# The last block of a two-layer matmul: o5 as a fifth plain store, and o1 made on ScalarE

## Chip, cores, metric

One core of one Trainium2 chip. The metric is the time of the whole kernel on the device, in microseconds; lower is better. I also read the **tail** in each trace: the span minus the end of the last matmul. It leaves out the small drift of everything before. Spans are printed to 0.1 us, so a tail is good to about 0.1 us.

## The reference

```python
batch, m, k, h, n = 16, 512, 768, 3072, 768
def reference(x, w1, b1, w2):
    y = np.matmul(x, w1) + b1
    y = np.maximum(y, 0)
    return np.matmul(y, w2).astype(np.float32)
```

## The kernel before

The 8192 rows are worked through in 16 blocks, 8 for each half of the hidden dimension. The second product of a block consists of 20 small products ("mm") whose results are combined into eight outputs o0 to o7 of 128x768 floats (0.39 MB) each. In the first 8 blocks an output is stored; in the last 8 the second half's sum has to be added to what is stored. Usually the DMA does that: GpSimd issues an accumulating store. In the very last block, four outputs (`LAST`) go another way: the stored rows are fetched early, GpSimd adds them to a kept sum in SBUF, and the output then leaves as a plain store.

```python
SECOND = (            # ("mm", product, bank pair, start), (engine, to, bank pair, sign, kept, its sign)
    # [cut]
    ("mm", 10, 2, False),
    ("DVE", "q1", 2, 1, "s5", 1),
    ("DVE", "o5", 1, -1, "s2", 1),
    ("mm", 14, 0, False),
    ("ACT", "s4", 0, -1),
    ("mm", 9, 3, False),
    ("DVE", "q1", 3, -1, "s4", 1),
    ("DVE", "o7", 1, 1, "s1", -1),
    ("mm", 17, 2, False),
    ("DVE", "o4", 2, 1, "s5", 1),
    ("mm", 0, 0, False),
    ("DVE", "o1", 0, 1, "s3", -1),
    ("mm", 7, 3, False),
    ("DVE", "o6", 3, -1, "s4", 1),
)
# [cut]
    LAST = {"o7": ("s1", -1, 3), "o4": ("s5", 1, 15), "o1": ("s3", -1, 12), "o6": ("s4", 1, 16)}

    def fetch_last(self, to):
        slot = list(self.LAST).index(to)
        self.nc.sync.dma_start(out=self.x_outputs(slot), in_=self.rows_of(self.NIT - 1, to))

    def add_last(self, to):
        slot = list(self.LAST).index(to)
        name, sign, _ = self.LAST[to]
        s = self.s[:, int(name[1])].rearrange("p (a n) -> p a n", a=2)
        self.nc.gpsimd.tensor_tensor(out=s, in0=s, in1=self.x_outputs(slot),
                                     op=ALU.add if sign > 0 else ALU.subtract)
# [cut: total(), which combines one result]
            if final and to == SECOND[-1][1]:                     # o6, in two halves
                for j, queue in enumerate((nc.scalar, nc.sync)):
                    nc.vector.tensor_tensor(out=o[:, j], in0=at(kept)[:, j], in1=ps[:, j],
                                            op=ALU.subtract)
                    queue.dma_start(out=self.rows_of(it, to)[:, j], in_=o[:, j])
                return
# [cut]
            if to[0] == "o":
                rows = self.rows_of(it, to)
                if it < self.NSB or (final and to in self.LAST):
                    nc.sync.dma_start(out=rows, in_=o)
                else:
                    nc.gpsimd.dma_start(out=rows, in_=o, accum_op=ALU.add)
```

## Time and profile before

| | before |
|---|---|
| time, median of 3 runs | 880.64 us (880.54 to 880.95) |
| span of the profiled run | 879.4 us |
| last matmul ends | 870.62 us |
| last store issued | 872.89 us |
| DMA at full rate until | 876.0 us |
| DMA queues drained (SP's wait for the last store is over) | 878.5 us |
| tail (span less last matmul) | 8.8 us |

From the last matmul on, the table is the tail in order of time. Before it TensorE is at 98%. The lines of the page, of the timeline and of the DMA stretches are in the prediction below.

### The profile page before, as it was taken

The page shows a single profiled execution, that of the slowest core. Times are in us where ns is not written, and L with a number is a line of the kernel's source. Part 1 is how long each engine was busy: PE and PEld are TensorE (multiplying, and loading weights), DVE is VectorE, ACT ScalarE, POOL GpSimd, SP SyncE. Part 2 cuts the span into 40 slices and gives each one's busy share as a digit, 9 for nine tenths or more (in the row PEclk, how much of TensorE's full clock was granted, in tenths as well). Part 3 has the DMA queues.
Part 4 walks back from the last instruction along what each step waited for, and adds up shares of the span by engine and source line. Part 5 has one row for each costly group of instructions (what it writes and reads, how often), then busy time and mean ns, then how long its engine had stood idle before and what let it go on. Part 6 is the DMA issues. An engine that isn't in the chain of part 4 may idle for free.

```text
span 879.4 us, 12571 instructions
## 1 busy us (share of the span) xinstructions
PE 866.2 (98%) x4677; PEld 458.1 (52%) x4677; DVE 619.3 (70%) x1082; ACT 518.8 (59%) x791; POOL 193.3 (22%) x173
## 2 busy tenths in 40 slices
PE   8999999999999999999999999999999999999996
PEld 6454554645545455554545545455454555545453
DVE  2897857767677666866799676665866668566684
ACT  4865757768576776766356576775626345363541
POOL 6310150503305041040200402103030130401214
PEclk9999999999999999999999999999999999999998
DMA  9999598796977959549551837548263573726607
GB/s 206 197 224 273 109 251 219 136 264 148 280 161 190 255 91 268 122 179 337 224 180 55 129 102 167 89 137 133 86 118 67 149 121 126 102 43 162 108 1 146
DMA packets 121429, 139.68 MB, mean 159 GB/s; under 512 B 67196, under 2 KB 114836, under 8 KB 117524
## 3 DMA queue, kind: packets, MB, share of 16 engines
q0 software_dynamic: 49584, 44.83, 35.9%
q1 hardware_dynamic: 71312, 93.01, 32.3%
q10 hardware_dynamic: 468, 1.00, 0.4%
q8 instruction: 38, 0.62, 0.3%
q14 instruction: 27, 0.22, 0.1%
HBM read 73.74 MB, written 77.66 MB: 172 GB/s over the span
## 4 chain that ended last, share of the span: by engine, by line
PE 50%; issue 35%; POOL 9%; DVE 3%; DMA 2%; ACT 0%; POOLq 0%; DVEq 0%; ACTq 0%
PE ps L536 25%; PE ps L633 25%; POOL out_dram L685 8%; DVE v L338 1%; DMA v<-in_w_dram 1%; DMA w1s<-in_w_dram 1%; DVE y L468 1%; POOL s L618 1%; POOL w1s L277 1%; DVE o L678 0%; ACT ps L672 0%; DVE w1s L285 0%; DVE ps L678 0%; DVE x L678 0%; DVE x L391 0%
## 5 line engine op out<-in xcount | busy, mean ns | idle before, releaser
L633 PE MATMUL ps<-v,y 128*128 128x384 f16 x2560 | 424.6, 326 | 1.0 <-ACT ps L672 0.6
L536 PE MATMUL ps<-x,w1s 128*128 128x512 f16 x1890 | 415.6, 379 | 0.0
L633 PEld LDWEIGHTS <-y 128*128 128x128 f16 x2560 | 249.6, 98 | 173.0 <-ACT y L553 2.5
L536 PEld LDWEIGHTS <-w1s 128*128 128x128 f16 x1890 | 184.8, 98 | 218.6 <-issue 0.9
L544 ACT ACTIVATE s<-ps,b1y 128x512 f32<-128x512 f32 x210 | 142.1, 686 | 149.7 <-PE ps L536 69.2
L468 DVE TENSOR_TENSOR y<-y 128x512 f16<-128x512 f16 x512 | 203.2, 422 | 33.5 <-ACT y L553 26.0
L548 DVE CUSTOM_DVE_ANT_0 y<-ps,s 128x512 f16<-128x512 f32 x210 | 144.8, 690 | 102.8 <-PE ps L536 70.9
L672 ACT ACTIVATE s<-ps 128x768 f32<-128x768 f32 x96 | 77.7, 809 | 119.0 <-PE ps L633 106.7
L685 POOL DMA_DIRECT2D out_dram<-o x58 | 71.2, 1363 | 327.9 <-DVE o L678 327.9
L678 DVE TENSOR_TENSOR s<-ps,s 128x768 f32<-128x768 f32 x96 | 90.1, 952 | 11.6 <-ACT s L672 5.6
L678 DVE TENSOR_TENSOR o<-s,ps 128x768 f32<-128x768 f32 x54 | 51.3, 950 | 48.3 <-PE ps L633 25.9
L553 ACT ACTIVATE y<-ps,b1y 128x512 f16<-128x512 f32 x90 | 61.8, 687 | 39.7 <-PE ps L536 39.7
L678 DVE TENSOR_TENSOR o<-ps,s 128x768 f32<-128x768 f32 x55 | 51.3, 953 | 37.0 <-ACT s L672 35.1
L394 POOL TENSOR_TENSOR x<-x 128x3072 f16<-128x3072 f16 x7 | 42.0, 6004 | 65.2 <-DVE x L391 52.8
L382 ACT ACTIVATE scrap<-xn 128x768 f16<-128x768 f16 x60 | 50.3, 838 | 0.8
L277 POOL DMA_DIRECT2D x<-in_w_dram x12 | 10.1, 848 | 180.5 <-PE ps L536 92.9
L559 ACT ACTIVATE ps<-ps,b1y 128x512 f32<-128x512 f32 x60 | 39.5, 659 | 10.3 <-PE ps L536 7.6
L553 ACT ACTIVATE y<-ps 128x512 f16<-128x512 f32 x60 | 35.8, 597 | 0.0
L346 ACT ACTIVATE scrap<-scrap 128x1536 f16<-128x1536 f16 x24 | 35.4, 1476 | 0.1
L672 ACT ACTIVATE ps<-ps 128x768 f32<-128x768 f32 x32 | 25.5, 797 | 10.0 <-PE ps L633 8.4
L486 PE MATMUL ps<-x,w1s 128*128 128x512 f16 x132 | 28.8, 379 | 0.4 <-DVE x L441 0.2
L369 POOL DMA_DIRECT2D xn<-in_x_dram x15 | 11.5, 764 | 65.9 <-ACT scrap L382 65.2
(69 smaller groups left out, 288.5 us busy)
## 6 DMA issues: line engine op xcount, KB each, us to landing
out_dram<-o POOLq DMA_DIRECT2D x58, 384.0 KB, 5.9
out_dram<-o SPq DMA_DIRECT2D x51, 384.0 KB, 4.8
xd<-x SPq DMA_DIRECT2D x8, 1536.0 KB, 6.1
x<-xd SPq DMA_DIRECT2D x8, 1536.0 KB, 8.2
xn<-in_x_dram POOLq DMA_DIRECT2D x15, 768.0 KB, 7.2
xd<-x SPq DMA_DIRECT2D x7, 1152.0 KB, 8.0
x<-xd SPq DMA_DIRECT2D x7, 1152.0 KB, 5.3
out_dram<-x SPq DMA_DIRECT2D x16, 384.0 KB, 5.9
```

Source lines behind the costliest of these rows:

```text
L382: self.nc.scalar.activation(out=self.junk(self.K), in_=rows, func=ACTF.Square, accum_out=self.stat[:, i:i + 1])
L394: (self.nc.gpsimd if it > 1 else self.nc.vector).tensor_tensor(out=x[:, a21:self.XS2 + 1:self.XS2 - a21], in0=x[:, a21:self.XS1 + 1:self.X ...
L468: self.nc.vector.tensor_tensor(out=pair(*outs), in0=pair(*ins0), in1=pair(*ins1), op=ALU.add if sign > 0 else ALU.subtract)
L536: nc.tensor.matmul(ps, lhsT=w[:, slot, k, :], rhs=x[:, xslot, k, :], start=(start and k == 0), stop=(k == 2), skip_group_check=True)
L544: nc.scalar.activation(out=kept(name), in_=ps, func=ACTF.Identity, bias=bias)
L548: nc.vector._custom_dve(TENSOR_ADD_SAT, out=self.y_of(self.TP * half + t, m), in0=self.two(ps), in1=self.two(kept(name)), s0=F_MAX, s1=0.0)
L553: nc.scalar.activation(out=self.y_of(self.TP * half + t, m), in_=self.two(ps), func=ACTF.Relu, **kw)
L559: nc.scalar.activation(out=g["b"], in_=g["a"], func=ACTF.Identity, bias=bias1)
L633: nc.tensor.matmul(self.ps[:, 2 * q + j, 0:NH], lhsT=self.y[:, U_OF[p], m0:m0 + P], rhs=self.v[:, V_OF[p], s, :], start=(start and s == 0) ...
L672: nc.scalar.activation(out=o, in_=ps, func=ACTF.Copy, scale=float(sign))
L678: nc.vector.tensor_tensor(out=o, in0=a, in1=b, op=ALU.add if sign == kept_sign else ALU.subtract)
L685: nc.gpsimd.dma_start(out=rows, in_=o, accum_op=ALU.add)
```

## The change

Its intent: o5 becomes a fifth output that leaves by a plain store, so that no accumulating DMA stands among the last stores; and o1's kept sum is put into its banks of PSUM, the memory that TensorE writes to, before its last product, so that idle ScalarE can copy o1 out and store it from its own queue, and VectorE has one output less at the end.

```diff
-    LAST = {..., "o6": ("s4", 1, 16)}
+    LAST = {..., "o6": ("s4", 1, 16),
+            "o5": ("s2", 1, 5)}
@@ total()
-                    nc.sync.dma_start(out=rows, in_=o)
+                    (nc.scalar if final and to == "o1" else nc.sync).dma_start(out=rows, in_=o)
@@ second()
-        for what in SECOND:
+        order = list(SECOND)
+        if final:
+            at_s4 = order.index(("ACT", "s4", 0, -1))
+            order.insert(at_s4 + 1, ("DVE", "q0", 0, 1, "s3", -1))
+            order[order.index(("DVE", "o1", 0, 1, "s3", -1))] = ("ACT", "o1", 0, 1)
+        for what in order:
@@ plan()
-            put("m1", NIT - 1, 1, 6, self.fetch_last, to)
+            put(*(("m2", NIT - 1, 0, 1) if to == "o5" else ("m1", NIT - 1, 1, 6)),
+                self.fetch_last, to)
```

More of the change, by code (lines that the diff above doesn't have):

```diff
@@ L604, in x_outputs @@
         return o.rearrange("p (a n) -> p a n", a=2)
-    LAST = {"o7": ("s1", -1, 3), "o4": ("s5", 1, 15), "o1": ("s3", -1, 12), "o6": ("s4", 1, 16)}
+    LAST = {"o7": ("s1", -1, 3), "o4": ("s5", 1, 15), "o1": ("s3", -1, 12), "o6": ("s4", 1, 16),
+            "o5": ("s2", 1, 5)}
     def fetch_last(self, to):
```

## The prediction

> **What bounds the kernel now.** I read the page first, then the end of the timeline, then the waits there, then the DMA by stretches. The page says that TensorE is busy for 98% of the span, and the two costliest groups, the matmuls of the two products, have almost no idle time before them:
>
> ```profile
> PE 866.2 (98%) x4677; PEld 458.1 (52%) x4677; DVE 619.3 (70%) x1082; ACT 518.8 (59%) x791; POOL 193.3 (22%) x173
> ...
> L633 PE MATMUL ps<-v,y 128*128 128x384 f16 x2560 | 424.6, 326 | 1.0 <-ACT ps L672 0.6
> L536 PE MATMUL ps<-x,w1s 128*128 128x512 f16 x1890 | 415.6, 379 | 0.0
> ```
>
> The change touches nothing before the last of the 16 blocks' second product, so 843 us of the 879.4 us span are out of its reach, and within that product TensorE is fed without a gap (2.00 of 2.00 us in each stretch from 845 us to 869 us). What is left to gain is what comes after the last matmul. The timeline of the last 16 us shows it (start, duration, engine, line, what is written and read, count, idle time before):
>
> ```profile
> 864.95 1.21 POOL L685 DMA_DIRECT2D out_dram<-o  x1 [1.64 <-DVE o L678]
> 865.52 0.81 ACT L672 ACTIVATE s<-ps 128x768 f32<-128x768 f32 x1 [1.85 <-PE ps L633]
> 865.76 0.95 DVE L678 TENSOR_TENSOR o<-s,ps 128x768 f32<-128x768 f32 x1
> 866.85 0.96 DVE L678 TENSOR_TENSOR ps<-s,ps 128x768 f32<-128x768 f32 x1
> 867.01 1.20 POOL L685 DMA_DIRECT2D out_dram<-o  x1 [0.85 <-DVE o L678]
> 867.77 4.04 POOL L618 TENSOR_TENSOR s<-s,x 128x768 f32<-128x768 f32 x2
> 867.91 0.96 DVE L678 TENSOR_TENSOR o<-ps,s 128x768 f32<-128x768 f32 x1
> 868.90 3.41 SPq L683 DMA_DIRECT2D out_dram<-o  x3
> 870.09 1.82 DVE L678 TENSOR_TENSOR o<-ps,s 128x768 f32<-128x768 f32 x2 [1.22 <-POOL s L618]
> 871.85 1.02 DVE L666 TENSOR_TENSOR o<-s,ps 128x384 f32<-128x384 f32 x2
> 872.43 0.38 ACTq L668 DMA_DIRECT2D out_dram<-o  x1
> 872.89 0.34 SPq L668 DMA_DIRECT2D out_dram<-o  x1
> ```
>
> The last matmul ends at 870.6 us. GpSimd is the late one: it issues output o5 as an accumulating DMA at 867.01, and only then begins its two sums (o4's at 867.77, o6's after it, ending at 871.81). VectorE waits 1.22 us for the first, then does o4 and o1, then the two halves of o6, which end at 872.87. The last store goes out at 872.89, and 6.5 us later the span ends. These 6.5 us are DMA:
>
> ```profile
> 871.00:872.00 1.00, 0.00 (x0) 0.00 (x0) 1.00 (x3) 0.00 (x0) 0.81 (x1) 1.00 1.14 244
> 872.00:873.00 1.00, 0.00 (x0) 0.00 (x0) 0.87 (x2) 0.00 (x0) 0.00 (x0) 0.85 1.12 393
> 873.00:874.00 1.00, 0.00 (x0) 0.00 (x0) 0.00 (x0) 0.00 (x0) 0.00 (x0) 0.50 1.01 370
> 874.00:875.00 1.00, 0.00 (x0) 0.00 (x0) 0.00 (x0) 0.00 (x0) 0.00 (x0) 0.50 1.04 370
> 875.00:876.00 1.00, 0.00 (x0) 0.00 (x0) 0.00 (x0) 0.00 (x0) 0.00 (x0) 0.50 0.96 349
> ```
>
> The last two columns are the DMA share and GB/s. The engines are full until 876 at about 370 GB/s, then some lag until 877.5; the queues drain at 878.5 and the span ends 0.9 us later. By queue over the last 14 us (packets, MB, share of 16 engines' time):
>
> ```profile
> q0 software_dynamic: 544, 0.79, 40.9%
> q1 hardware_dynamic: 960, 1.38, 28.1%
> ```
>
> q0 holds GpSimd's two accumulating DMAs (o0, o5): 0.409 x 14 / 2 = 2.9 us of all 16 engines for one output. q1 holds plain stores of 1.38 MB: 0.281 x 14 = 3.9 us, so 1.1 us for one output of 0.39 MB. In half-microsecond stretches, o7's plain store, issued at 868.90, has its first packets only after 871, and the accumulating queue holds the engines until then. So the end is bound twice over: by o6's sum reaching VectorE late, and by four plain stores (1.57 MB) that queue up behind o5's accumulation.
>
> **What the Trainium skill says.** DMA: Bandwidth & Descriptors, section "SWDGE vs HWDGE vs iDMA", has an accumulating DMA go through GpSimd and a plain one through SP or ACT; the trace agrees (all L685 are POOL). The same page, "Issuing engines are not separate DMA queues", says that transfers from any issuer end on the same 16 engines, so that a second issuer saves only issuing time. The trace agrees: while both hardware queues run, the rate stays at 370 GB/s. I therefore give the second queue no bandwidth. The same page, "Anatomy of one DMA", gives some 2 us of fixed cost, mostly the receipt of the last write; here it is about 1 us from the last packets (877.5) to the drain, and from issue to first data 1.1 to 1.5 us (ACT's store issued at 872.43 has first packets between 873.5 and 874). SBUF — State Buffer, "Who interferes with whom", says that a VectorE instruction with two SBUF inputs and a GpSimd one that reads SBUF block each other, while one with a single SBUF input does not. The trace agrees: an f16 sum beside GpSimd's sum at 848.4 took 2.03 us in place of 0.4, while the PSUM-reading sum at 867.91 kept its 0.96.
>
> **The change part by part.** Orders and semaphores are read from the built programs.
> - Removed: the accumulating issue of o5 on GpSimd (1.2 us there, 2.9 us of all DMA engines).
> - Added early: one fetch of o5's rows (0.39 MB), free to go when the last block's first x-quarter is read, about 839 us, when DMA is idle; and one GpSimd sum of 1.9 to 2.3 us after step 5, near 854.5 us, where GpSimd is idle until 856.8. It may block the one f16 sum at 854.38 for 1.6 us; VectorE is idle 2.49 us before 859.0 and absorbs it. Cost: 0.
> - Added late: VectorE's sum of s3 into bank pair 0, between o5 and "q1 = s4 - q3". Sums with nothing to wait for start 0.87 us apart (854.71, 855.58), so it runs 866.65 to 867.6, q1 to 868.5, o7 868.6 to 869.5 (0.65 us later than now). The matmuls of product 0 now wait for it: 20 products of 1.31 us end at 870.62, so product 0 is due at 868.0 and product 7, which waits for q1, at 869.3. Slack 0.4 and 0.8 us: no TensorE cost.
> - Moved: o1 leaves VectorE (0.95 us) for ScalarE, idle since 866.3: product 0 ends at 869.3, so o1 is made 869.45 to 870.25 (0.80 us) and issued by ACT near 870.3, in place of 871.9.
> - GpSimd: o4's sum no longer stands behind o5's issue. It starts about 865.9 (after "q1 = q2 + s5" at 865.73) and ends near 868.1; o6's starts when q1 is made, 868.55, and takes 2.27: 870.8.
> - VectorE's end: o4 869.4 to 870.4, o6's halves 870.85 to 871.4 and to 871.9. Now 872.87: about 1.0 us earlier.
> - DMA: o5's plain store at 866.8 shares the engines with the rest of o0's accumulation and is through about 871. Then o7 (869.6), o1 (870.3), o4 (870.45), o6 (871.5, 871.95). First data of o7 is due 1.3 us after its issue, 870.9, where now it is about 871.6; four outputs at 370 GB/s are 4.25 us, so full rate ends near 875.2 in place of 876.0. Gain 0.7 to 0.8.
>
> The two ends (last issue 1.0 earlier, engines free 0.75 earlier) leave about 0.9 us; the laggards after 876 may shrink a little too, since those still full of accumulation at 871 are gone. 880.64 - 0.95 = 879.7 us.
>
> **The rivals.** (1) The drain hides it: five plain stores still need 5.3 us of the engines after 866.8, and if the o0 accumulation (landing about 870.3) holds o5's store back, the four last stores start no earlier than now. For it: o7 waited 2.6 us behind o5's accumulation today. Against it: the plain store takes 1.7 us less of the engines. Result 880.3 to 880.6. (2) The new wait on TensorE: if VectorE's sum into the banks ends after 868, the last products shift. For it: the slack is only 0.4 us, against semaphore delays of about 0.1. Even a 0.5 us shift of TensorE would be covered in part, as o6's sum arrives 0.2 us after its last matmul; result about 880.0. (3) More gain: with no accumulation in the last 6 us, the last store lands in the least time seen for such stores (2.4 us to landing against 4.3 to 5.1 here). Then the end comes at 871.95 + 3 + 1 = 876, which would need 1.57 MB faster than 370 GB/s; I allow up to 2 us in all, 878.7.
>
> **Range and chances.** The centre is 879.7. Rival 1 sets the upper end, 880.4; rival 3 the lower, 878.8. Two per cent would be 17.6 us, twice all the time after the last matmul (8.8 us), so faster is out of reach; slower would need a stall nowhere in the orders. Same 0.98, faster 0.01, slower 0.01.
>
> **What would show it.** Last matmul unmoved at 870.6 (right for the slack); the new sum into ps ending before 868; ScalarE's o1 near 869.5; no VectorE wait on GpSimd for o4; o6's halves ending near 871.9; the first plain-store packets before 871 and full rate ending near 875.2; the span near 878.4. Wrong if the last matmul comes later, if o6 still waits past 871.5 for GpSimd, or if VectorE ends earlier but the DMA drain doesn't.

## The result, and the profile after

The changed kernel takes 879.85 us (879.60 to 880.07, 6 runs) where the one before took 880.91 (880.54 to 881.34, 6 runs): 1.06 us less. The ratio is 0.9988 with a 95% interval of 0.9975 to 1.0001, so within 2% beyond doubt, and by the times alone not quite clear of zero. A ratio is the mean time of one kernel's fast runs over that of the other's of the same rounds, so not quite the ratio of the medians quoted.

The trace is clearer: span 878.2 us, last matmul at 870.71 (845.85 + 24.86, against 870.62), so the tail went from 8.8 to 7.5 us.

The end of the timeline of the changed kernel (start, duration, engine, line, out and in, count, idle time before). L679 is what L678 was, L619 what L618 was, L684 and L669 the stores:

```profile
865.97 2.13 POOL L619 TENSOR_TENSOR s<-s,x 128x768 f32<-128x768 f32 x1
866.78 0.96 DVE L679 TENSOR_TENSOR ps<-ps,s 128x768 f32<-128x768 f32 x1
866.90 3.97 SPq L684 DMA_DIRECT2D out_dram<-o  x3
867.65 0.95 DVE L679 TENSOR_TENSOR ps<-s,ps 128x768 f32<-128x768 f32 x1
868.64 1.82 DVE L679 TENSOR_TENSOR o<-ps,s 128x768 f32<-128x768 f32 x2
868.74 1.82 POOL L619 TENSOR_TENSOR s<-s,x 128x768 f32<-128x768 f32 x1 [0.64 <-issue]
869.45 0.81 ACT L673 ACTIVATE o<-ps 128x768 f32<-128x768 f32 x1 [3.03 <-PE ps L634]
870.29 0.50 ACTq L684 DMA_DIRECT2D out_dram<-o  x1
870.60 1.02 DVE L667 TENSOR_TENSOR o<-s,ps 128x384 f32<-128x384 f32 x2
871.18 0.37 ACTq L669 DMA_DIRECT2D out_dram<-o  x1
871.64 0.34 SPq L669 DMA_DIRECT2D out_dram<-o  x1
```

GpSimd begins o4's sum at 865.97, not 867.77, and VectorE no longer waits for that sum. The new sum into the banks is the one at 866.78. ScalarE makes o1 at 869.45. o6's halves end at 871.62, not 872.87, and the last store goes out 1.25 us earlier.

The stretches of the changed kernel (from left: window, its length, busy us and count of TensorE's matmuls, its weight loads, VectorE, ScalarE and GpSimd; TensorE's clock, DMA share, GB/s; the share is the time of all packets over that of 16 engines and can pass 1):

```profile
869.00:870.00 1.00, 1.00 (x8) 0.61 (x7) 1.00 (x2) 0.55 (x1) 1.00 (x1) 1.00 1.09 289
870.00:871.00 1.00, 0.71 (x5) 0.20 (x2) 0.87 (x2) 0.26 (x1) 0.56 (x1) 1.00 0.96 355
...
874.00:875.00 1.00, 0.00 (x0) 0.00 (x0) 0.00 (x0) 0.00 (x0) 0.00 (x0) 0.62 0.89 313
875.00:876.00 1.00, 0.00 (x0) 0.00 (x0) 0.00 (x0) 0.00 (x0) 0.00 (x0) 0.50 0.28 36
```

Full rate begins near 869.5 in place of 872 and ends near 874.8 in place of 876.0. The queues over the last 12.2 us of the changed kernel (q0 is GpSimd's, q1 SP's, q10 ScalarE's):

```profile
q1 hardware_dynamic: 960, 1.38, 33.2%
q0 software_dynamic: 272, 0.39, 24.4%
q10 hardware_dynamic: 416, 0.59, 13.6%
```

One accumulating output is left on q0 (o0: 0.244 x 12.2 = 3.0 us of all engines), and five plain ones are on q1 and q10. The drain ends at 877.3 and the span at 878.2.

Two explanations fit this: GpSimd, and so VectorE and the last issue, came free earlier; or the DMA engines did. And two halves of the change could have done it. The experiments take these apart.

### The profile page after: what moved, and what is told of

The parts are those of the page before. It is cut to its first block, busy times and chain, and to the rows that moved or that the text cites. A ratio compares the mean times of both kernels' runs of the same rounds, so it can differ in the third digit from the quotient of the medians.

```text
span 878.2 us, 12581 instructions
## 1 busy us (share of the span) xinstructions
PE 867.0 (99%) x4677; PEld 458.9 (52%) x4677; DVE 619.5 (71%) x1082; ACT 519.6 (59%) x792; POOL 194.0 (22%) x173
## 4 chain that ended last, share of the span: by engine, by line
PE 91%; DVE 4%; DMA 2%; POOL 1%; issue 1%; ACT 1%; DVEq 0%; POOLq 0%; ACTq 0%
PE ps L536 46%; PE ps L634 45%; DVE y L468 1%; DVE v L338 1%; DMA v<-in_w_dram 1%; DMA w1s<-in_w_dram 1%; POOL w1s L277 1%; DVE o L679 0%; DVE y L548 0%; POOL s L619 0%; ACT ps L673 0%; DVE ps L679 0%; ACT s L544 0%; ACT y L553 0%; DVE w1s L285 0%
## 5 line engine op out<-in xcount | busy, mean ns | idle before, releaser
L679 DVE TENSOR_TENSOR s<-ps,s 128x768 f32<-128x768 f32 x96 | 90.2, 954 | 11.5 <-ACT s L673 5.6
L679 DVE TENSOR_TENSOR o<-s,ps 128x768 f32<-128x768 f32 x54 | 51.4, 952 | 48.3 <-PE ps L634 25.9
L679 DVE TENSOR_TENSOR o<-ps,s 128x768 f32<-128x768 f32 x54 | 50.4, 953 | 35.7 <-ACT s L673 35.1
L277 POOL DMA_DIRECT2D x<-in_w_dram x12 | 10.1, 848 | 180.8 <-PE ps L536 92.6
```

What stands on the lines that cost most here:

```text
L679: nc.vector.tensor_tensor(out=o, in0=a, in1=b, op=ALU.add if sign == kept_sign else ALU.subtract)
```

## The experiments

Eleven builds ran, two of them repeats, in three groups of one chip each, all with five timed runs and one trace. The tail is worked out as above.

| kernel | time, us (range) | ratio, 95% interval | span | tail |
|---|---|---|---|---|
| before | 880.64 (880.54 to 880.95) | | 879.4 | 8.8 |
| changed | 879.85 (879.60 to 880.07) | 0.9988 (0.9975 to 1.0001) | 878.2 | 7.5 |
| group 1: after_again | 879.81 (879.56 to 879.98) | 0.9987 (0.9974 to 1.0001) | 878.3 | 7.4 |
| o5_plain | 879.26 (879.07 to 879.54) | 0.9982 (0.9968 to 0.9996) | 877.6 | 7.0 |
| act_o1 | 880.57 (880.15 to 880.77) | 0.9995 (0.9982 to 1.0009) | 878.9 | 8.2 |
| one_queue | 879.59 (879.52 to 880.09) | 0.9986 (0.9973 to 1.0000) | 878.0 | 7.3 |
| group 2: accum_last | 882.40 (882.01 to 882.68) | 1.0019 (1.0005 to 1.0032) | 881.0 | 10.1 |
| no_o7_store (wrong) | 879.55 (879.34 to 879.94) | 0.9989 (0.9975 to 1.0002) | 877.8 | 7.2 |
| pool_late | 879.71 (879.68 to 879.86) | 0.9991 (0.9977 to 1.0004) | 878.1 | 7.4 |
| o7_late | 879.84 (879.81 to 880.02) | 0.9992 (0.9978 to 1.0006) | 878.3 | 7.7 |
| group 3: o5_plain_again | 879.34 (879.27 to 879.52) | 0.9983 (0.9970 to 0.9997) | 877.8 | 7.1 |
| two_queues | 879.60 (879.30 to 879.90) | 0.9986 (0.9973 to 1.0000) | 877.9 | 7.2 |
| o0_plain | 879.31 (879.12 to 879.64) | 0.9983 (0.9969 to 0.9996) | 877.7 | 7.0 |

The kernel before ran beside each group: medians 880.93, 880.71 and 880.77, single runs from 879.82 to 881.55. Group 2 held neither the changed kernel nor o5_plain, and group 3 not the changed kernel; where I compare across groups, I rest on the tail more than on the times.

### after_again: the changed kernel as yardstick

No edit.

> The changed kernel once more, on the chip of this group, as the yardstick. It should be 0.9 to 1.2 us under the kernel before (ratio near 0.9988), with the same end as in its first trace: VectorE's last half of o6 done near 871.6, last store issued near 871.6, span 878.2.

It came as expected: 879.81 us, tail 7.4. The two traces of the changed kernel differ by 0.1 us in the tail, and so do those of o5_plain, below; with the rounding of the spans I read nothing into less than 0.2.

### o5_plain: only the first half of the change

```diff
+            "o5": ("s2", 1, 5)}          # and its fetch; SECOND and the queues as before
```

> The kernel before with o5 alone turned into a plain store (its fetch and its GpSimd sum too); o1 stays on VectorE and all stores on the SP queue. Theory 1 (the gain comes from taking the accumulating DMA of o5 away): GpSimd's sums for o4 and o6 start near 866.0 and 868.0, VectorE ends o6 near 871.6, span 878.2 to 878.4, so at least 0.8 us of the gain of about 1.1. Theory 2 (the gain comes from ScalarE taking o1 off VectorE): VectorE, with one more sum behind product 0, ends at 872.5 or later and the span stays above 879.0.

Theory 1 holds, and by more than it said: this half alone is faster than the whole change. Its ten runs in two groups lie at 879.07 to 879.54, the eleven of the whole change at 879.56 to 880.07. Timeline of this version, VectorE (o7, o4 and o1, then o6's halves):

```profile
867.93 2.69 DVE L679 TENSOR_TENSOR o<-ps,s 128x768 f32<-128x768 f32 x3
870.54 1.01 DVE L667 TENSOR_TENSOR o<-s,ps 128x384 f32<-128x384 f32 x2
```

VectorE makes o1 too and ends o6 at 871.55, no later than with ScalarE's help (871.62). It needed none: its three outputs stand there without a gap, and product 0 was due then anyway. The stretches of this version:

```profile
870.00:871.00 1.00, 0.65 (x4) 0.20 (x2) 1.00 (x3) 0.00 (x0) 0.00 (x0) 1.00 1.07 401
...
874.00:875.00 1.00, 0.00 (x0) 0.00 (x0) 0.00 (x0) 0.00 (x0) 0.00 (x0) 0.50 0.76 244
```

In 870 to 871 the engines move 401 GB/s, against 355 in the changed kernel, and by 874 to 875 there is less left to move (244 against 313).

### act_o1: only the second half

```diff
-            "o5": ("s2", 1, 5)}          # o5 accumulates again; the rest of the change stays
```

> The changed kernel with o5 accumulated as before: only the kept sum put into the banks, o1 made on ScalarE and stored from its queue. Theory 1: VectorE still waits for GpSimd (o4 near 870.1, o6 near 871.8), the last store goes out near 872.9, and the span stays within 0.3 us of 879.4. Theory 2: VectorE ends about 0.9 us earlier and the span is 878.5 or less.

VectorE's part came as theory 1 said: o4 at 870.21 after a wait for GpSimd, o6's halves at 871.97, last issue 873.01. The span was 878.9, and the 0.3 us around 879.4 that I gave it was too narrow; the tail is 0.6 us shorter than before. The median is 0.36 us under that of the kernel before, with an interval on both sides of 1: unclear. The trace says how a gain could come without an earlier last issue: o1's store went out at 870.31 in place of 871.94, so the engines had it in their queue sooner. The halves do not add: 1.7 to 1.8 us (tail) for the first, 0.6 for the second, 1.3 to 1.4 for both.

### one_queue: the changed kernel with o1's store on SP

```diff
-                    (nc.scalar if final and to == "o1" else nc.sync).dma_start(out=rows, in_=o)
+                    nc.sync.dma_start(out=rows, in_=o)
```

> The changed kernel with o1's store issued by SP in place of ScalarE's queue; nothing else. If the second queue adds no bandwidth (theory 1): span within 0.3 us of the changed kernel's 878.2, DMA rate in the full stretch still about 370 GB/s. If the second queue carries the gain (theory 3): the rate or the start of o1's data suffers and the span goes back by 0.5 us or more.

Span 878.0, tail 7.3: the second queue carries none of the gain. The rate at 871 to 874 was 354 to 366 GB/s, against 353 to 374 with two.

### pool_late: VectorE and the last issue as late as before, the DMA work as after

```diff
+        if to == "o6":                    # a useless sum ahead of o6's, in add_last()
+            f = self.x.rearrange("p a k m -> p a (k m)")
+            self.nc.gpsimd.tensor_tensor(out=f[:, 6, 0:1024], in0=f[:, 6, 0:1024],
+                                         in1=f[:, 7, 0:1024], op=ALU.add)
```

> The changed kernel with a useless GpSimd sum of 1.5 to 2 us ahead of o6's sum, so that o6's halves reach VectorE about 1.3 us later and nothing else moves. If the end follows the last issue: the span grows by 1.3 us, to 879.5. If it follows the drain: the engines have four other outputs to write until about 873.7, and o6's data could start only near 874.2, so it grows by 0.4 to 0.8 us.

This is the run that decides. Its timeline:

```profile
867.73 2.43 POOL L620 TENSOR_TENSOR x<-x 128x1024 f16<-128x1024 f16 x1
...
869.81 2.10 POOL L623 TENSOR_TENSOR s<-s,x 128x768 f32<-128x768 f32 x1
...
871.94 1.02 DVE L671 TENSOR_TENSOR o<-s,ps 128x384 f32<-128x384 f32 x2 [1.50 <-POOL s L623]
...
872.99 0.34 SPq L673 DMA_DIRECT2D out_dram<-o  x1
```

GpSimd is late again, VectorE waits 1.50 us for it, and the last store goes out at 872.99, 2.29 us after the last matmul; in the kernel before it was 2.27. What the change had won for o6 and for the last issue is taken back, and the span is 878.1, the tail 7.4, the time 879.71 (1.00 under the kernel before of its group; the whole change 1.06): nothing is lost. Both theories expected a loss, the drain theory 0.4 to 0.8 us. Its own stretches show why there is none:

```profile
873.00:874.00 1.00, 0.00 (x0) 0.00 (x0) 0.00 (x0) 0.00 (x0) 0.00 (x0) 1.00 1.11 381
874.00:875.00 1.00, 0.00 (x0) 0.00 (x0) 0.00 (x0) 0.00 (x0) 0.00 (x0) 1.00 0.84 282
```

There is no gap: the engines were still at full rate with the other outputs when o6 arrived, so its lateness is hidden entirely. **The earlier o6 and the earlier last store were worth nothing; the gain lies in when the DMA engines come free.** One thing the run leaves as the change made it: o4's store goes out at 870.47 and o1's at 870.27, in place of 871.07 and 871.94. Whether GpSimd's earlier sum for o4 helped, by having that store queued in time, no run tests by itself; o7_late, below, shows that a late store can cost.

### accum_last: the other way round

```diff
+                elif final and to == "o5":
+                    self.late = (rows, o)
@@ plan()
+        put("m2", NIT - 1, 0, 16, self.store_late)   # the same accumulating store, behind o6's sum
```

(store_late() issues the held store.)

> The kernel before with one move: GpSimd issues o5's accumulating DMA behind its two last sums in place of ahead of them. This frees GpSimd as the plain store did and leaves the DMA work where it was. If the end follows VectorE's last sum (6.5 us from the last issue to the end): VectorE ends near 871.5 and the span is near 878.1. If the end follows the drain of the DMA engines: VectorE ends near 871.5 all the same, but the accumulation, issued near 870, now falls among the last stores; 4.2 us of plain stores and 2.9 us of accumulation from about 869.7 end near 876.8, so the span is 879.4 to 880.2, no better than before.

The kernel before, with GpSimd freed and the accumulation left. VectorE ends o6 at 871.78 and the last store goes out at 871.80, as early as in the changed kernel. The kernel is 1.7 us slower than before (882.40 against 880.71 in its group; interval clear of 1), of which the tail shows 1.3. The direction is the drain theory's, the size over its 880.2. Its stretches show the cost of an accumulation among the last stores, full share at a low rate; a smaller part of the loss is a gap ahead of the plain stores (share 0.24 from 869.5 to 870.0), where the accumulation had stood before:

```profile
872.00:873.00 1.00, 0.00 (x0) 0.00 (x0) 0.00 (x0) 0.00 (x0) 0.00 (x0) 1.00 1.03 137
873.00:874.00 1.00, 0.00 (x0) 0.00 (x0) 0.00 (x0) 0.00 (x0) 0.00 (x0) 1.00 0.99 217
```

### no_o7_store: one store less

```diff
+                if final and to == "o7":
+                    return
```

> The changed kernel with the store of o7 left out: its rows keep the first half's sum, so the result is wrong on purpose. It takes 0.39 MB, 1.06 us at 370 GB/s, from the last DMA work and nothing from any compute engine. If the end follows the drain: the span shortens by 0.7 to 1.1 us, to about 877.3. If it follows the last issue: it stays at 878.2 within 0.2.

Between the two: span 877.8, tail 0.2 to 0.3 us shorter than the two of the changed kernel. Taking out a whole output's 1.06 us gave less than a third of it, because the engines then ran dry:

```profile
870.00:871.00 1.00, 0.65 (x4) 0.19 (x2) 0.87 (x3) 0.19 (x1) 0.49 (x1) 1.00 0.46 169
```

o5 was nearly all written by 870.5, and o1's store, issued at 870.22, had its first packets only after 871. So the drain is not just a sum of bytes: it also counts whether a store is in the queue when the engines come free.

### o7_late: what the second half costs

The version with only o5 plain, with o7's store behind o4's.

```diff
+                if final and to == "o7":
+                    self.held = (rows, o)
...
+                    if final and to == "o4":
+                        nc.sync.dma_start(out=self.held[0], in_=self.held[1])
```

> The version with only o5 plain (0.5 us faster than the whole change), with o7's store issued right behind o4's, near 870.2 in place of 868.9; compute is the same. In the whole change the sum put into the banks makes o7 0.65 us later. If that lateness is what the ScalarE half costs: the span goes from 877.6 to 878.0 or more, time near 879.7. If the cost has another cause (the second queue, ScalarE itself): the span stays within 0.2 of 877.6.

o7's store goes out at 870.21 in place of 868.9; VectorE's last sum is where it was (871.49). Time 879.84 and span 878.3, as the first theory said. The stretch shows the hole:

```profile
870.00:871.00 1.00, 0.60 (x4) 0.15 (x2) 1.00 (x3) 0.00 (x0) 0.00 (x0) 1.00 0.72 261
```

A late o7 is enough to lose 0.5 us (0.6 to 0.7 in the tail, against the two traces of o5_plain in the other groups). In the whole change o7's store goes out at 869.6, because the sum into the banks stands ahead of it on VectorE. The hole there is smaller (355 GB/s, share 0.96), so this run shows the mechanism, not that all of the 0.5 us is owed to it.

### o5_plain_again and two_queues

No edit for the first; for the second, on the same version:

```diff
-                    nc.sync.dma_start(out=rows, in_=o)
+                    (nc.scalar if final and to == "o1" else nc.sync).dma_start(out=rows, in_=o)
```

> The version with only o5 plain, once more, as the yardstick of this group and to see whether its lead over the whole change holds on another draw: about 879.3 us (ratio 0.998), span near 877.6. If it was a lucky chip or build: near 879.8.

> The version with only o5 plain, with o1's store (still made on VectorE) issued from ScalarE's queue as in the whole change. If the second queue is neutral: within 0.2 us of the yardstick. If two rows with work make the drain slower: 0.2 us or more above it. If they add bandwidth: below it, with more than 400 GB/s in the full stretch.

The lead of o5_plain held (879.34). With o1's store on the second queue it was 879.60. That is 0.26 us more, over the 0.2 from which I would have called the second queue slower, but single runs overlap and the tails differ by 0.1 us. Together with one_queue (0.22 us better with one queue, ranges overlapping too): two queues gain nothing; whether they cost 0.2 us stays open.

### o0_plain: no accumulating store issued after 861 us

```diff
+            "o5": ("s2", 1, 5), "o0": (None, 1, None)}
+            if final and to == "q1" and q == 2 and engine == "ACT":
+                nc.vector.tensor_tensor(out=o, in0=ps, in1=self.x_outputs(5), op=ALU.add)
+            elif kept is None:
```

(Cut: o0's fetch, placed as o5's, and no GpSimd sum for it.)

> The version with only o5 plain, with o0 made a plain store as well: its rows are fetched early and VectorE, idle there, adds them where ScalarE had only copied the seed of bank pair 1. No accumulating DMA is left after 861. Drain theory: o5's data no longer waits for o0's accumulation (starts near 868.2 in place of 869.3), but the four last stores are then limited by their own issue (o7 868.9), so full rate ends near 874.0 in place of 874.2 and the span shortens by 0 to 0.3 us. If the engines that lag by some 2 us at the very end owe it to accumulation behind them: it shortens by 1 us or more.

879.31 us, no different from o5_plain. Full rate does end a little earlier (112 GB/s in 874 to 875 in place of 244), but the queues drain at 876.8 as there (876.7). A whole accumulation less gained nothing, because the engines then ran dry ahead of o7, whose store goes out at 868.96:

```profile
869.00:870.00 1.00, 1.00 (x8) 0.59 (x6) 1.00 (x2) 0.00 (x0) 0.83 (x1) 1.00 0.14 52
```

Some engines still lag by about 2 us, so the lag is not owed to accumulations behind them. Which engines these are, the profile doesn't show; the cause stays open.

## Why the prediction was right

Predicted 879.7 us (878.8 to 880.4), measured 879.85; the predicted gain was 0.95 us, the measured one 1.06. Its steps:

- **TensorE has slack for the new wait.** Right: the sum into the banks ran 866.78 to 867.74 (predicted 866.65 to 867.6), and the last matmul stayed at 870.7.
- **GpSimd, VectorE and ScalarE.** Right within 0.3 us: o4's sum 865.97 to 868.10 (865.9 to 868.1), o1 at 869.45 (869.45), o7 868.64 (868.6), o6's halves done at 871.62 (871.9).
- **"The end is bound twice over: by o6's sum reaching VectorE late, and by four plain stores."** Half wrong. pool_late put o6's sum and the last issue back to where they were and lost nothing; the queued stores bound the end. The prediction averaged two gains, 1.0 and 0.75 us, of which the first was worth zero. That the number held all the same is luck: the two were nearly equal, and the second was too small.
- **The engines come free 0.75 us earlier.** The right term, too small: 1.2 us (full rate to 874.8 in place of 876.0). I let o7's data start at 870.9 behind an o5 that would be through "about 871", and counted from there. In the trace full rate began near 869.5, when o0's accumulation ended. By 870.5, 245 of the 272 packets of one output had gone out on SP's queue, so by my estimate o5 was through near 870.6 and o7's data followed with hardly a gap. Four outputs at 370 GB/s from there end near 874.85, which is what was measured.
- **The laggards (engines still busy after full rate ends) may shrink.** They didn't: from the end of full rate to the drain it is 2.5 us in both kernels, and o0_plain kept them too. They had been given only about 0.05 us.
- **"Moved: o1 leaves VectorE".** I gave this a gain and never asked how the end would look without it; my own sum starts from o7's data at 870.9, which the 0.65 us delay sets. o5_plain shows that this half is worth less than nothing beside the first: without it the kernel is 0.5 us faster. o7_late shows that a late o7 can cost as much.
- **Rival 1, the drain hides it.** It was right that everything depends on the drain, wrong that the stores start no earlier: plain-store data started between 869 and 869.5, not after 871 as before. Rivals 2 and 3 did not come. (Rival 3's sum was loose: it quotes 2.4 us to landing and then adds 3.)
- **The fixed cost of a DMA.** The page section that I set beside SP's and ACT's stores describes a DMA issued by GpSimd, so my "about 1 us" doesn't test its figure. Nothing in the forecast rests on it.

Not settled: what exactly makes up the 0.5 us between o5_plain and the whole change, how much of o5_plain's gain is DMA work saved and how much is o4 queued in time, and why some engines end 2 us after the others.

## What to carry to other kernels

At the end of a kernel, ask first when the DMA engines come free and only then which compute engine ends last: an earlier last store was worth nothing here while earlier ones were still being written. Take accumulating DMAs out of the last stores, as long as the engines are what the stores wait for (o5 here, but no longer o0), and order the work so that each store is queued when the one before it ends. Two sound changes can share one gain: test each alone, for one of them may cost.

## What the Trainium skill lacked or had wrong

- DMA: Bandwidth & Descriptors, on what an accumulating DMA costs the engines: the page names who may issue it and gives no rate. Here 0.39 MB took 2.9 to 3.0 us of all 16 engines accumulated and 1.1 us as a plain store, and accum_last lost 1.7 us with one such transfer moved among the last stores.
- The same page, "Queues, rings and completion order", says that each engine serves its queue rows in turn, packet by packet. These runs show less sharing than that suggests: in the changed kernel o5's plain store, issued at 866.90, had no packet before 869 while o0's accumulation ran, and in the kernel before o7's had 2 packets against 67 between 871.0 and 871.5. With the engines nearly idle (o0_plain) a store issued at 864.75 had its first packets between 865.5 and 866.0. No trace shows whether the waiting store's work had reached the engines, so how it is held back stays open.
- No page that I read has this: a store that is queued late leaves a hole that the total of the bytes doesn't show. With one output of 1.06 us fewer, the tail shortened by only 0.2 to 0.3 us (no_o7_store); with one store issued 1.3 us later, the time grew by 0.5 us (o7_late).
